# Row sums of |x − y| on one core: the final wait on the output store moves from SyncE to TensorE

## The chip, the cores and the metric

The kernel runs on one core of one Trainium2 chip. The metric is the device time of one execution in microseconds (us). The time of a kernel is the median of several executions without the profiler. One further execution is recorded by the hardware profiler; the profile and the trace come from that one.

## The reference

Two arrays of 1024 rows by 4096 columns are subtracted, and the absolute differences are summed along each row:

```python
def reference(x, y, axis):          # x, y: (1024, 4096) float32, axis = -1
    return np.sum(np.abs(x - y), axis=axis).astype(np.float32)
```

The output is 1024 numbers, 4 KB. The inputs are 33.5 MB.

## The kernel before

The 1024 rows are spread over the 128 partitions, so that each partition owns K = 8 rows. Rows 0 to 3 of a partition go through the buffers `xa` and `yb`; rows 4 to 7 go through `xb` and once more `yb`. VectorE (DVE) subtracts in place (L134), and ScalarE (ACT) takes the absolute value and sums along the row (L143) into one column of `ro`, the 128 by 8 tile of results. Rows 5 and 6 are handled in two halves each, and the last row in five pieces of 1728, 1024, 640, 384 and 320 columns, so that little work is left when the last bytes arrive. The last piece is done by VectorE alone: a subtraction (L175), and a sum over absolute values (L177) that adds the partial sums of the other pieces as well.

All input transfers but one are issued on SyncE's (SP's) queue, in the order of the code. The one exception, the first half of y, is issued by ScalarE (L114). Before each transfer that overwrites a row of `yb`, SP waits until VectorE has subtracted the row that stands there (L117 and L124).

The order on each engine is written out by hand. The helper `put` takes every instruction out of the block in which it was made. It either places it ahead of the program's first barrier (the first loads) or keeps it in the list `rest`, which is appended at the very end of the program, after the last barrier that the program itself has. So the program's barriers are all over within the first 2.4 us, and after that each engine simply runs its own list to the end. TensorE (PE) has nothing in that list: after the last barrier its program is over.

Every semaphore that the kernel counts up is also set back at the end by an instruction that waits for its final value and subtracts it. On VectorE `take_back` does this (L139). On SP three steps end the program:

- L183 and L184: SP waits until `s_end` has reached 7, that is, until all sums stand in `ro`, and issues the store of `ro` to the output. The store adds 16 to the semaphore `s_out` when it has landed.
- L185: SP sets `s_end` back.
- L186: SP waits until `s_out` has reached 16, and sets it back. Nothing follows it on SP.

Of the kernel before, what the change touches and what calls it, by code (L numbers as in the profile page):

```python
# [18 lines left out]
class Entry:  # L19
# [26 lines left out]
    def put(self, emit, before=None):  # L46

        nc = self.nc
        hook = nc.inst_callbacks[-1]
        lower = nc._always_lower_symbolic_ap  # L50
        nc.remove_inst_callback(hook)
        nc._always_lower_symbolic_ap = False
        n = len(nc.cur_bb.bb.instructions)
        try:
            emit()
        finally:
            nc._always_lower_symbolic_ap = lower
            nc.push_inst_callback(hook)
        here = nc.cur_bb.bb.instructions
        main = nc.main_func.blocks[0].instructions  # L60
        while len(here) > n:
            mine = here.pop(n)
            if before is None:
                self.rest.append(mine)
            else:
                first = next(i for i, x in enumerate(main) if x.engine == mine.engine and x.opcode == before)
                main.insert(first, mine)
# [3 lines left out]
def kernel(ctx, tc, x, y, axis, out):  # L71
    nc = tc.nc
# [11 lines left out]
    put = entry.put  # L84
# [24 lines left out]
    s_out = nc.alloc_semaphore("s_out")  # L109
# [73 lines left out]
    put(lambda: nc.sync.wait_ge(s_end, done))  # L183
    put(lambda: nc.sync.dma_start(out=orr, in_=ro).then_inc(s_out, 16))  # L184
    put(lambda: nc.sync.wait_ge(s_end, done).then_inc(s_end, -done))  # L185
    put(lambda: nc.sync.wait_ge(s_out, 16).then_inc(s_out, -16))  # L186


# [33 lines left out]
```

## Time and profile before

| what | us |
|---|---|
| median of 3 executions | 84.15 (84.14 to 84.20) |
| the profiled execution, its own time | 84.31 |
| its span, first to last recorded instruction of the kernel | 83.0 |
| VectorE busy | 36.4 |
| ScalarE busy | 31.6 |
| GpSimd (POOL) busy | 0.2 |
| mean rate of the transfers over the span | 404 GB/s |

The span begins with the first instruction that the kernel itself holds and ends with its last one. The device time of the same execution is longer by 1.3 us, which lies around the span; the page has no row for it. TensorE has no row of busy time because it does no matmul. An engine's letter with a q behind it (SPq, PEldq) means the engine's sequencer: waits, semaphore updates and the issuing of transfers.

### The profile page before, as it was taken

What the parts mean: (1) busy time and instruction counts of PE and PEld (TensorE: products, weight loads), DVE (VectorE), ACT (ScalarE), POOL (GpSimd) and SP (SyncE); (2) the same over time, 40 slices, a digit from 0 to 9 for tenths busy, and PEclk for the clock granted to TensorE, in tenths of its full rate; (3) what the DMA queues carried; (4) which work ended last, traced back from release to release, by engine and by line L of the source; (5) the groups of instructions that cost most, each with busy time, mean ns of one, the idle gap of its engine ahead of it and who ended that gap; (6) DMA issues with size and microseconds to landing.
All of it is one profiled execution on the core that took longest, in us unless ns stands there. A gap on an engine that the chain in (4) does not pass through costs nothing.

```text
span 83.0 us, 115 instructions
## 1 busy us (share of the span) xinstructions
DVE 36.4 (44%) x16; ACT 31.6 (38%) x27; POOL 0.2 (0%) x4
## 2 busy tenths in 40 slices
DVE  0000000000000000000199999999279898999772
ACT  0600000000000000000000979889790599999990
POOL 0000000000000000000000000000000000000000
DMA  6996899979798999998888999869999989999950
GB/s 126 411 735 269 379 569 498 434 332 553 332 521 363 490 395 403 498 403 379 379 379 379 450 663 403 379 253 395 474 395 419 466 379 419 423 411 409 405 207 2
DMA packets 2592, 33.56 MB, mean 404 GB/s; under 512 B 416, under 2 KB 928, under 8 KB 1696
## 3 DMA queue, kind: packets, MB, share of 16 engines
q1 hardware_dynamic: 2448, 25.17, 72.3%
q10 hardware_dynamic: 144, 8.39, 23.4%
HBM read 33.55 MB, written 0.00 MB: 404 GB/s over the span
## 4 chain that ended last, share of the span: by engine, by line
DMA 63%; DVE 17%; SPq 11%; issue 6%
DMA yb_rows<-in_y_dram 63%; DVE xa_rows L134 16%; SPq L122 6%; SPq L125 4%; DVE last_piece L175 1%; DVE ro_sums L177 1%
## 5 line engine op out<-in xcount | busy, mean ns | idle before, releaser
L134 DVE TENSOR_TENSOR xa_rows<-xa_rows,yb_rows 128x4096 f32<-128x4096 f32 x4 | 17.4, 4422 | 41.1 <-DMA yb_rows<-in_y_dram 41.1
L143 ACT ACTIVATE xa_rows<-xa_rows 128x4096 f32<-128x4096 f32 x4 | 14.5, 3616 | 43.8 <-DVE xa_rows L134 43.8
L134 DVE TENSOR_TENSOR xb_rows<-xb_rows,yb_rows 128x2048 f32<-128x2048 f32 (+5 forms) x9 | 17.9, 2016 | 3.6 <-DMA yb_rows<-in_y_dram 3.5
L143 ACT ACTIVATE xb_rows<-xb_rows 128x2048 f32<-128x2048 f32 (+1 forms) x5 | 11.2, 2245 | 3.0 <-DVE xb_rows L134 3.0
L143 ACT ACTIVATE abs_piece<-xb_rows 128x1728 f32<-128x1728 f32 (+3 forms) x4 | 3.8, 944 | 0.0
L143 ACT ACT_TABLE_LOAD x1 | 1.3, 1283 | 2.4 <-PEq L217 2.4
L143 ACT ACTIVATION_READ_ACCUMULATOR xb_rows<-xb_rows 128x1 f32 x5 | 0.9, 187 | 0.0
L143 ACT ACTIVATION_READ_ACCUMULATOR xa_rows<-xa_rows 128x1 f32 x4 | 0.7, 186 | 0.0
L143 ACT ACTIVATION_READ_ACCUMULATOR abs_piece<-xb_rows 128x1 f32 x4 | 0.7, 186 | 0.0
L175 DVE TENSOR_TENSOR last_piece<-xb_rows,yb_rows 128x320 f32<-128x320 f32 x1 | 0.5, 493 | 0.3 <-DMA yb_rows<-in_y_dram 0.3
L177 DVE TENSOR_REDUCE ro_sums<-last_piece 128x1 f32<-128x324 f32 x1 | 0.5, 491 | 0.0
L169 DVE TENSOR_REDUCE ro_sums<-half_sums 128x2 f32<-128x4 f32 x1 | 0.1, 150 | 0.0
L203 POOL MEMSET const-bfloat16-1.0<- 128x1 bf16 x1 | 0.1, 101 | 0.0
L203 POOL MEMSET const-uint8-127<- 128x1 uint8 x1 | 0.1, 101 | 0.0
L203 POOL MEMSET const-float32-0.0<- 128x1 f32 x1 | 0.1, 98 | 0.2 <-issue 0.2
L203 POOL MEMSET const-float32-1.0<- 128x1 f32 x1 | 0.1, 98 | 0.0
## 6 DMA issues: line engine op xcount, KB each, us to landing
xa_rows<-in_x_dram SPq DMA_DIRECT2D x1, 6144.0 KB, 36.9
xb_rows<-in_x_dram SPq DMA_DIRECT2D x1, 6144.0 KB, 53.3
yb_rows<-in_y_dram SPq DMA_DIRECT2D x3, 2048.0 KB, 15.5
xa_rows<-in_x_dram SPq DMA_DIRECT2D x1, 2048.0 KB, 17.0
xb_rows<-in_x_dram SPq DMA_DIRECT2D x1, 864.0 KB, 17.8
yb_rows<-in_y_dram SPq DMA_DIRECT2D x1, 864.0 KB, 15.9
xb_rows<-in_x_dram SPq DMA_DIRECT2D x1, 512.0 KB, 16.7
yb_rows<-in_y_dram SPq DMA_DIRECT2D x1, 512.0 KB, 17.5
```

The costliest lines, as they stand in the source:

```text
L122: put(lambda: nc.sync.dma_start(out=xb[:, H - 1, c], in_=xr[:, K - 1, c]).then_inc(s_piece[i], 16))
L125: put(lambda: nc.sync.dma_start(out=yb[:, H - 1, c], in_=yr[:, K - 1, c]).then_inc(s_piece[i], 16))
L134: put(lambda: nc.vector.tensor_sub(out=tx, in0=tx, in1=ty).then_inc(s_sub, 1))
L143: put(lambda: nc.scalar.activation(tx if out is None else out, tx, ABS, accum_out=to).then_inc(sem, 1))
L169: put(lambda: nc.vector.reduce_sum(out=ro[:, K - 3:K - 1], in_=half, axis=AX).then_inc(s_end, 1))
L175: put(lambda: nc.vector.tensor_sub(out=last[:, n_part:n_part + w], in0=tx, in1=ty).then_inc(s_end, 1))
L177: put(lambda: nc.vector.reduce_sum(out=ro[:, K - 1:K], in_=last, axis=AX, apply_absolute_value=True).then_inc(s_end, 1))
L203: nc = _bacc.Bacc("TRN2", target_bir_lowering=False, num_devices=1)
```

## The change

The last instruction, the wait for the store with the setting back of `s_out`, is given to TensorE. The store itself stays where it is, on SP's queue. SP's last instruction is then L185. TensorE's list, which was empty after the barriers, holds this one wait.

```diff
     put(lambda: nc.sync.wait_ge(s_end, done))
     put(lambda: nc.sync.dma_start(out=orr, in_=ro).then_inc(s_out, 16))
     put(lambda: nc.sync.wait_ge(s_end, done).then_inc(s_end, -done))
-    put(lambda: nc.sync.wait_ge(s_out, 16).then_inc(s_out, -16))
+    put(lambda: nc.tensor.wait_ge(s_out, 16).then_inc(s_out, -16))
```

In the built program nothing else differs: VectorE, ScalarE and GpSimd have the same instructions in the same order, SP has one fewer at its end, and TensorE one more at its end.

## The prediction

> **What bounds the kernel now.** I read the page's head, then the chain that ended last in order of time, then SP's own waits, and at the end the semaphore records of the trace, since the change touches only the last microsecond. The chain first (columns: start in us, length in us, what):
>
> ```profile
> 67.72 12.70 DMA yb_rows<-in_y_dram
> 80.42 0.02 issue
> 80.45 0.50 DVE last_piece L175
> 80.95 0.02 issue
> 80.97 0.49 DVE ro_sums L177
> ```
>
> The transfers set the time until 80.42, and two VectorE steps follow. Neither is touched by the change. After 81.46 only the store is left. From the timeline of the last stretch, SP's waits, the issues of transfers and the row of line L186:
>
> ```profile
> 81.49 0.35 SPq L184 DMA_DIRECT2D out_dram<-ro_sums  x1
> ```
> ```profile
> SPq L186 <- SPq L186: 1.1, 1, 1.1
> ```
> ```profile
> out_dram<-ro_sums SPq DMA_DIRECT2D x1, 4.0 KB, 1.4
> ```
> ```profile
> L186 SPq EVENT_SEMAPHORE  x1: 17/17/17, 83.0 to 83.0; - x1
> ```
>
> The store is issued at 81.49, lands 1.4 us later, and SP has waited 1.1 us for it when L186 ends the span. So the question is what follows once the store has landed. The span is 83.0 us and the same execution took 84.31: 1.31 us lie around the span, and the page says nothing of them.
>
> The trace does. It records updates of semaphores too, also by instructions that are not the kernel's. Semaphore 2 is none of the kernel's. Its updates from the kernel's own barriers on, with the last instruction of an engine that fits (us from the span's start; who made each is my reading):
>
> ```
>  2.592  first: TensorE or GpSimd, whose last instructions start at 2.306 and 2.253
> 80.931  ScalarE, whose last instruction ended at 80.817
> 80.969  GpSimd or TensorE, idle since 2.6
> 81.858  VectorE, whose last instruction started at 81.655
> 83.116  SP, whose L186 started at 82.957 and ended at 82.974
> 83.160  83.198  83.233  83.280                  four more, back down
> 84.068 84.102 84.140 84.184 84.208 84.306 84.344 84.378 84.425   the same again
> ```
>
> Five updates going up, four coming back: a chain in which each engine waits for the one ahead. SP is the last link, since only its update waits for the store. Between 83.237 and 83.843 some 230 other semaphores are updated once each, in five ranges of about fifty; the lowest range (7 to 53) starts at 83.497, last of the five, and ends at 83.843. Then a second chain of nine.
>
> [...] the second chain runs from 84.068 to 84.425, 357 ns for 8 hops. [...] here the 17 ns of L186 stand for a step of 159 ns up to SP's update.
>
> **The change, part by part.**
>
> Removed: L186 on SP. SP's list then ends with L185 at 81.89, so its closing steps (159 ns from L186's start to its chain update) go under the flight of the store. This saves nothing by itself, because SP may update only after VectorE, which waits for the engines ahead of it, and one of these is now TensorE.
>
> Added: one wait on TensorE. Nothing of the kernel is queued behind it, nobody in the kernel waits for it, no transfer is issued or moved, and TensorE is idle from 2.6 on. Its price comes from the barriers at the start, where both sequencers wait for the same release. The rows of line L217, filtered by engine:
>
> ```profile
> L217 PEldq EVENT_SEMAPHORE  x2: 51/51/51, 2.0 to 2.3; - x2
> ```
> ```profile
> L217 SPq EVENT_SEMAPHORE  x2: 17/17/17, 2.0 to 2.3; - x2
> ```
>
> The same wait takes 51 ns on TensorE and 17 on SP. In the third barrier the release is updated at 2.278, SP's wait starts at 2.294 and TensorE's at 2.306: TensorE reacts 28 ns after the update, SP 16. From the start of that wait to TensorE's chain update at 2.592 it is 286 ns, if the first link is TensorE. A second sign of its pace: in the second barrier its next instruction starts 151 ns after the wait, SP's 91.
>
> Moved: the place in the chain at which everyone waits for the store. Step by step, on the records of the profiled execution:
>
> 1. The sixteenth increment of `s_out` is at 82.940. [...] the records show sixteen increments, 82.740 to 82.940. The store stays as it was, so this stays.
> 2. TensorE's wait starts 28 ns later, 82.968 (SP's: 82.957, 17 ns after). **+0.011**
> 3. Its chain update comes 286 ns after that, 83.254 (SP's: 159 ns, 83.116). **+0.127**, together +0.138.
> 4. Before, four hops were left when the late engine updated: 83.280 − 83.116 = 0.164. Now, with TensorE first, all eight are left; the undisturbed chain shows them with 0.357. **+0.193**
> 5. From the first engine's release (83.280) to the last update (84.425) it is 1.145 us[...]. The lowest range ends last in both kernels and starts last, so this part moves as a block. **0**[...].
>
> Sum: 0.138 + 0.193 = **+0.331 us**, of which only about 0.045 (11 + 51 − 17 ns) shows as a longer span. The profiled execution goes from 84.31 to about 84.64. The median of 84.15 stands 0.16 below the profiled execution; I add the sum to it: **84.48**.
>
> Bounds of what I can't see. If the first link is GpSimd and TensorE the third, six hops are left: 0.044 + 0.024 + 0.098 + 0.038 + 0.034 + 0.047 = 0.285, so +0.121 in step 4 and +0.26 in all; I take first, since of the two TensorE is the slower and the first link reacts slowest in the way down (47 ns against 38). Step 3 could be as short as SP's 159 ns (then +0.20) and, with a second delay of 151 ns, as long as 437 (then +0.48).
>
> **The rivals.**
>
> *The time ends before the closing steps.* The last update is at 84.425 and the execution took 84.31, so one end of the metric isn't where my records begin or stop. If all of the 1.31 us lay ahead of the span, only the 0.045 us of the longer span would count: 84.20. Against it: nine updates follow within 84.07 to 84.43, hard to see left out of an 84.31 that starts near zero. For it: the page shows neither end.
>
> *SP's own closing work is what the tail consists of.* Then it would start at 81.91 rather than at 82.97, under the store, and the end would come sooner. It decides where SP's share of the tail, once it runs under the store, is longer than TensorE's by over 0.17 + 0.045. The gain is limited by L186's wait of 1.07 us; with half of that, less 0.045, it gives 84.15 − 0.49 = 83.66. Against it: after SP's update four hops follow that others make, and the highest range of semaphores, next to SP's place in the chain, is done at 83.330, half a microsecond ahead of the lowest.
>
> *The barrier is a count, not a chain.* Then only step 2 and step 3 count: +0.138, 84.29. Against it: gaps of 34 to 47 ns in the way down, and ScalarE's late update at 80.931, which drew the next 38 ns behind it.
>
> That the change doesn't do what it says is not open here: the built program has the wait on TensorE and nothing else moved.
>
> **How the numbers follow.** The chain with TensorE first or third: 0.80, between +0.20 and +0.48, likeliest +0.33. A count: 0.06, +0.14. The metric without the closing: 0.09, +0.05. SP's closing as the bound: 0.05, at 83.66. A measurement of this kernel can tell about 0.2%, 0.17 us, from no change. The chain is slower throughout; the count lies below that line and, with its own spread (0.1 to 0.25), gives 0.03 to each side of it. So faster 0.05, same 0.12, slower 0.83. The range runs from 84.20, which takes in the two small cases, to 84.62, just short of the longest step 3.
>
> **What would show it.** Right: L186 on TensorE with 51 ns, ending the span at about 83.02; SP's last instruction at 81.9; the updates of semaphore 2 not as 2.59, 80.93, 80.97, 81.86 and five late ones, but all nine after 83.2, within 0.36 us. Step 3 is read off the distance from the wait's start to the first of the nine, step 4 off the nine, step 5 off the distance from the ninth to the last. Wrong: one or more updates still ahead of the store beside a time that hasn't moved (TensorE is late in the chain), a store that lands later or sooner than 1.4 us, or nine late updates beside an unmoved time, which would put the metric's end before them.

## The result and the profile after

| | before | after |
|---|---|---|
| median, us | 84.15 (84.00 to 84.20, 6 executions) | 84.54 (84.39 to 84.73, 6 executions) |
| ratio | | 1.0052, 95% interval 1.0035 to 1.0068 |
| the profiled execution, us | 84.31 | 84.73 |
| its span, us | 82.97 | 83.07 |
| instructions in the span | 115 | 115 |

The change costs 0.39 us, about half a per cent. The six executions of the changed kernel include the profiled one, which was the longest; without it their median is 84.51. The span grew by only 0.09 us, and 0.05 of that is a later landing of the store; the rest of the cost lies behind the span. The end of the chain of waits in the kernel after (start in us, length in us, what):

```profile
67.76 12.71 DMA yb_rows<-in_y_dram
80.47 0.02 issue
80.49 0.51 DVE last_piece L175
81.00 0.02 issue
81.02 0.49 DVE ro_sums L177
```

These are the same steps with lengths equal within 0.01 us, all about 0.05 us later: the input transfers were that much later in this execution. SP's own waits, in the kernel after:

```profile
SPq L118 <- DVE xa_rows L134: 51.0, 3, 43.0
SPq L184 <- DVE ro_sums L177: 12.0, 1, 12.0
SPq L125 <- DVE xa_rows L134: 3.5, 1, 3.5
```

The row of L186 with its 1.1 us is gone from SP. The rows of lines L185 and L186 show where both now stand, and the timeline and the issues of transfers show the store:

```profile
L185 SPq EVENT_SEMAPHORE  x1: 17/17/17, 81.9 to 81.9; - x1
```
```profile
L186 PEldq EVENT_SEMAPHORE  x1: 51/51/51, 83.0 to 83.0; - x1
```
```profile
81.54 0.35 SPq L184 DMA_DIRECT2D out_dram<-ro_sums  x1
```
```profile
out_dram<-ro_sums SPq DMA_DIRECT2D x1, 4.0 KB, 1.4
```

SP is done at 81.9, TensorE's wait ends the span with its 51 ns, and the store takes 1.4 us as before. Nothing here accounts for 0.39 us. The records of semaphore 2, which is not the kernel's (its own instructions name only 96 to 112 in both traces), do (us from the span's start):

```
before   2.592 80.931 80.969 81.858 | 83.116 83.160 83.198 83.233 83.280
         84.068 84.102 84.140 84.184 84.208 84.306 84.344 84.378 84.425
after    | 83.346 83.380 83.419 83.463 83.486 83.584 83.624 83.658 83.704
         84.491 84.525 84.564 84.608 84.631 84.729 84.768 84.802 84.849
```

The bar marks the landing of the store, that is, the sixteenth increment of `s_out`: 82.940 before and 82.988 after. Before, four of the first nine updates had been made ahead of it. After, all nine follow it. From the landing to the last update it is 1.485 us before and 1.861 after, 0.376 more.

### The profile page after: what moved, and what is told of

Read it like the earlier page. It is cut to its first block, busy times and chain, and to the rows that moved or that the text cites. A ratio compares the mean times of both kernels' runs of the same rounds, so it can differ in the third digit from the quotient of the medians.

```text
span 83.1 us, 115 instructions
## 1 busy us (share of the span) xinstructions
DVE 36.4 (44%) x16; ACT 31.5 (38%) x27; POOL 0.2 (0%) x4
## 4 chain that ended last, share of the span: by engine, by line
DMA 63%; DVE 17%; SPq 10%; issue 6%
DMA yb_rows<-in_y_dram 63%; DVE xa_rows L134 16%; SPq L122 6%; SPq L125 4%; DVE last_piece L175 1%; DVE ro_sums L177 1%
```

## The experiments

The theory, read off the records above: at the end the engines pass a signal along a chain, TensorE first, then ScalarE, GpSimd, VectorE and SP, and back down to TensorE. What the wait on the store costs is set by the pace of the engine that holds it and by the links of the chain that are left after it. Rivals: using TensorE late costs by itself; only the engine's pace counts; or it costs that SP leaves while its store is under way.

The distances below are from the semaphore records of each profiled execution, in ns. An update is late when it is made after the landing of the store. "To wait" goes from the landing to the start of the wait on the store, "closing step" from there to the chain update that this engine makes, and "landing to last" from the landing to the very last update of semaphore 2; "against before" is the difference of the latter to the kernel before. Then come the medians' difference to before in the same comparison, and the ratio with its 95% interval.

The last column uses every execution. Each has a time, and a span that is known to 0.1 us. The difference of the two leaves out whatever happened ahead of the span's end, a late landing included. To its mean I add the part of the span that lies behind the landing in the profiled execution (34 ns before, 79 after), and subtract the same sum for the kernel before, 1.365 us over 102 executions in the later comparisons. The scatter of the difference makes the column good to some 0.02 us.

| run | late updates of the first nine | to wait | closing step | landing to last | against before | median, us | ratio | every execution, us |
|---|---|---|---|---|---|---|---|---|
| before | 5 | 17 | 159 | 1485 | | | | |
| after | 9 | 28 | 330 | 1861 | +376 | +0.39 | 1.0052 (1.0035 to 1.0068) | +0.39 |
| E1 TensorE early, SP waits | 5 | 17 | 148 | 1475 | −10 | −0.05 | 0.9997 (0.9985 to 1.0009) | −0.01 |
| E2 TensorE awake, and waits | 9 | 28 | 330 | 1862 | +377 | +0.41 | 1.0054 (1.0028 to 1.0079) | +0.37 |
| E3 ScalarE waits | 8 | 21 | 166 | 1654 | +169 | +0.19 | 1.0028 (1.0014 to 1.0042) | +0.18 |
| E4 VectorE waits | 6 | 27 | 204 | 1617 | +132 | +0.11 | 1.0014 (1.0001 to 1.0028) | +0.14 |
| E5 after again | 9 | 28 | 330 | 1863 | +378 | +0.43 | 1.0048 (1.0036 to 1.0060) | +0.39 |
| E6 TensorE, three more | 9 | 28 | 782 | 2313 | +828 | +1.14 | 1.0141 (1.0108 to 1.0173) | +0.82 |
| E7 SP, three more | 5 | 16 | 355 | 1680 | +195 | +0.23 | 1.0026 (1.0015 to 1.0037) | +0.20 |
| E8 TensorE and then SP | 9 | 28 | 330 | 1861 | +376 | +0.45 | 1.0059 (1.0045 to 1.0072) | +0.37 |
| E9 TensorE, two ahead | 9 | 28 | 286 | 1819 | +334 | +0.30 | 1.0037 (1.0021 to 1.0053) | +0.33 |
| E10 E6 again | 9 | 28 | 783 | 2315 | +830 | +0.80 | 1.0100 (1.0073 to 1.0127) | +0.81 |

In E6, E7 and E10 the closing step is counted from the first of the added waits; in E8 it is TensorE's. The two columns of differences that don't hold the landing, "against before" and "every execution", agree within 0.02 us in every row. The spare semaphore `s_pe` is allocated as in E1 wherever a later edit uses it; that line is not shown again.

**E1: TensorE has a last instruction, but an early one.** SP signals it after issuing the store.

```diff
+    s_pe = nc.alloc_semaphore("s_pe")
...
+    put(lambda: nc.sync.wait_ge(s_end, done).then_inc(s_pe, 1))
     put(lambda: nc.sync.wait_ge(s_end, done).then_inc(s_end, -done))
+    put(lambda: nc.tensor.wait_ge(s_pe, 1).then_inc(s_pe, -1))
     put(lambda: nc.sync.wait_ge(s_out, 16).then_inc(s_out, -16))
```

> The wait on the store is SP's again; TensorE gets a last instruction too, but one that is signalled by SP right after the store is issued, some 0.9 us before the store lands. Theory (a chain of engines, TensorE first, SP last; what counts is where in it the late engine stands, and how long its sequencer takes): TensorE's, ScalarE's, GpSimd's and VectorE's updates of semaphore 2 are all made by about 82.7 us, under the flight of the store, five updates are left after SP's wait, and the time is that of before, within 0.05 us. Rival (any last instruction on TensorE after its long idle time costs): +0.1 to +0.4 us, as in the changed kernel.

TensorE's row and SP's own wait in this run:

```profile
L188 PEldq EVENT_SEMAPHORE  x1: 51/51/51, 81.8 to 81.8; - x1
```
```profile
SPq L189 <- SPq L189: 1.0, 1, 1.0
```

TensorE's wait starts at 81.83 and makes its chain update at 82.159, and the next three follow by 82.275, all ahead of the landing at 82.836. SP still waits 1.0 us for the store. The time is that of before: an instruction on TensorE after its long idle time costs nothing here, where its chain update came 0.68 us ahead of the landing.

**E2: TensorE has worked just before.** As E1, but the wait on `s_out` is TensorE's too.

```diff
+    put(lambda: nc.sync.wait_ge(s_end, done).then_inc(s_pe, 1))
...
+    put(lambda: nc.tensor.wait_ge(s_pe, 1).then_inc(s_pe, -1))
-    put(lambda: nc.sync.wait_ge(s_out, 16).then_inc(s_out, -16))
+    put(lambda: nc.tensor.wait_ge(s_out, 16).then_inc(s_out, -16))
```

> As the changed kernel (TensorE waits for the store), but TensorE has one instruction ahead of it, signalled by SP just after the store is issued, so that its sequencer has worked within the last microsecond. Theory: still nine late updates in 0.36 us, so +0.33 to +0.38 us against before; what is open is the closing step of TensorE, 330 ns from its wait to its first update in the changed kernel against 286 in the kernel before, where it had just left a barrier: if the 80 us of waiting cost those 44 ns, it is 286 here, else 330. Rival (waking TensorE is most of the cost): the closing step falls by 0.15 us or more, and the time with it, to +0.2 us or less.

TensorE's two waits:

```profile
L188 PEldq EVENT_SEMAPHORE  x1: 51/51/51, 82.4 to 82.4; - x1
```
```profile
L189 PEldq EVENT_SEMAPHORE  x1: 51/51/51, 83.5 to 83.5; - x1
```

The second starts at 83.471, only 1.03 us after the first, and the chain update follows at 83.801. The closing step stayed at 330 ns. Long idleness of TensorE is not what costs, nor is it what separates 330 from 286.

**E3 and E4: the same wait on ScalarE, and on VectorE.** Each run has one of the two added lines.

```diff
-    put(lambda: nc.sync.wait_ge(s_out, 16).then_inc(s_out, -16))
+    put(lambda: nc.scalar.wait_ge(s_out, 16).then_inc(s_out, -16))    # E3
+    put(lambda: nc.vector.wait_ge(s_out, 16).then_inc(s_out, -16))    # E4
```

> The same wait is ScalarE's last instruction; TensorE has none. Theory: TensorE's update comes early again (2.6 us), eight come late. ScalarE's wait has SP's length, its closing step some 170 ns; from its update seven hops are left, 358 - 34 = 324 ns against SP's 164. So +0.15 us against before (the sequencer of ScalarE is fast: nearly all of it is its place). Rival (only the engine's own pace counts, not its place): within 0.03 us of before. Rival (it costs that SP leaves before its store has landed): the same 0.2 us on every engine other than SP, on top of the pace: +0.2.

> The same wait is VectorE's last instruction, behind the seven that set semaphores back. Theory: three updates come early, six late; VectorE's closing step is 203 to 231 ns (from its last instruction to its update in the kernel before), and from its update to the end of the chain it is 24 + 98 + 38 + 34 + 47 = 241 ns against SP's 164. So +0.13 us. Rival (pace alone): +0.055. Rival (SP leaving costs): +0.25.

The rows of the wait, first in E3, then in E4:

```profile
L186 ACTq EVENT_SEMAPHORE  x1: 17/17/17, 82.6 to 82.6; - x1
```
```profile
L186 DVEq EVENT_SEMAPHORE  x1: 21/21/21, 82.7 to 82.7; - x1
```

The first nine updates of semaphore 2 in these two runs, with the bar at the landing:

```
E3   2.583 | 82.788 82.827 82.870 82.893 82.991 83.031 83.065 83.112
E4   2.583 80.696 80.734 | 82.927 82.950 83.048 83.088 83.122 83.168
```

ScalarE's wait is as short as SP's, and its closing step only 7 ns longer. Yet the distance from landing to last is 169 ns longer, nearly all of it from ScalarE's update on: 324 ns to the end of the first pass (the first nine updates) instead of 164. That is place. Pace alone would have given 11 ns. VectorE is slower in pace but stands one link ahead of SP, and ends cheaper than ScalarE, at 132 ns. In E3 one of the nine updates came before the store, in E4 three, in the kernel after none: this shows the order TensorE, ScalarE, (GpSimd,) VectorE, SP. GpSimd has its place by elimination; the wait on GpSimd was not tried. The intervals of E3 and E4 overlap, so the medians would not tell the two apart. The last column, from 22 executions of each, does: +0.18 and +0.14.

**E5, E6, E7 and E10: the pace of the sequencer.** E5 is the changed kernel once more. E6 and E10 add three waits on TensorE that are satisfied once the store has landed. E7 adds the same three to the kernel before, on SP, ahead of SP's own last wait; all its lines have `nc.sync`.

```diff
+    for _ in range(2):
+        put(lambda: nc.tensor.wait_ge(s_out, 16).then_inc(s_pe, 1))     # E7: nc.sync
+    put(lambda: nc.tensor.wait_ge(s_pe, 2).then_inc(s_pe, -2))
     put(lambda: nc.tensor.wait_ge(s_out, 16).then_inc(s_out, -16))
```

> The changed kernel once more, beside before and the next three on one chip, for a narrower interval. Theory: +0.33 to +0.42 us; nine late updates of semaphore 2 within 0.36 us, the first 0.33 us after the start of TensorE's wait.

> The changed kernel with three more waits on TensorE that are satisfied as soon as the store has landed (two count a spare semaphore up, one sets it back). Theory (TensorE's sequencer lies open on the path after the store): three steps at the 151 ns that separate its instructions in the barriers, so 0.45 us more than the changed kernel, +0.83 us against before. Rival (the sequencer's pace is hidden, the cost is in the chain alone): no more than the changed kernel.

> The kernel before with the same three more waits, on SP. Theory: SP's sequencer lies open too, at 58 to 91 ns for a step: +0.17 to +0.27 us against before, clearly less than the same three on TensorE. Rival (time ends before the closing steps, or they are hidden): 0.

> The changed kernel with three more waits on TensorE after the landing, once more. In the first run of it the records from landing to last update gave 0.45 us more than the changed kernel, but the time was 1.1 us above before, with the store landing late. Theory (only the closing part differs, the late landing was chance): 2.313 us from landing to last update again, and a time of +0.7 to +0.95 us against before. Rival (the added waits delay the transfers too): the store lands about 0.5 us later than in the kernel before again, and +1.1 us or more.

The rows of the two waits of the loop, on TensorE in E10 and on SP in E7:

```profile
L188 PEldq EVENT_SEMAPHORE  x2: 51/51/51, 82.7 to 82.8; - x2
```
```profile
L188 SPq EVENT_SEMAPHORE  x2: 17/17/17, 83.2 to 83.2; - x2
```

TensorE's four waits start at 82.670, 82.821, 83.016 and 83.167: steps of 151, 195 and 151 ns. SP's start at 83.173, 83.247, 83.313 and 83.380: steps of 74, 66 and 67. TensorE's steps sum to 497 ns, but the closing step behind them is 286 instead of 330, so the three cost 0.45 us. SP's sum to 207 and cost 0.20 us: its closing step, too, is shorter here, 148 ns instead of 159. The medians of E10 (+0.80) and E7 (+0.23) agree with the records. The sequencers lie open on the path after the store, as expected. E6's median, +1.14, was more than the +0.83 of its records. What is too much lies ahead of the landing, which was at 83.506 in its profiled execution: its spans range from 83.2 to 84.2 us, while the time behind the landing is +0.82 over all six executions. E10, the same program, has the same distances within 2 ns, and landed the store at 82.642. So the added waits do not by themselves delay the transfers; why most executions of E6 had later transfers was not found.

**E8: SP stays until the store has landed, and TensorE is late as well.**

```diff
+    put(lambda: nc.tensor.wait_ge(s_out, 16).then_inc(s_pe, 1))
+    put(lambda: nc.sync.wait_ge(s_pe, 1).then_inc(s_pe, -1))
     put(lambda: nc.sync.wait_ge(s_out, 16).then_inc(s_out, -16))
```

> TensorE waits for the store and then signals SP, whose last instruction is the wait on the store as before; so SP does not leave before the store has landed, and TensorE is late as in the changed kernel. Theory: the chain begins with TensorE's update at the same distance from the store as in the changed kernel, SP is ready when the chain reaches it, so the time is that of the changed kernel within 0.05 us (+0.33 to +0.42). Rival (what costs is that SP leaves while its store is under way): at least 0.15 us less than the changed kernel.

The rows of TensorE's wait and of SP's last one in this run:

```profile
L187 PEldq EVENT_SEMAPHORE  x1: 51/51/51, 83.1 to 83.1; - x1
```
```profile
L189 SPq EVENT_SEMAPHORE  x1: 17/17/17, 83.2 to 83.2; - x1
```

SP ends last, as in the kernel before, and yet the distance from landing to last is the changed kernel's 1861 ns. That SP leaves early is not what costs.

**E9: where do TensorE's 44 ns come from?** Two short instructions ahead of TensorE's wait, both over before the store lands.

```diff
+    put(lambda: nc.sync.wait_ge(s_end, done).then_inc(s_pe, 1))
...
+    put(lambda: nc.tensor.wait_ge(s_pe, 1).then_inc(s_pe, 1))
+    put(lambda: nc.tensor.wait_ge(s_pe, 2).then_inc(s_pe, -2))
+    put(lambda: nc.tensor.wait_ge(s_out, 16).then_inc(s_out, -16))
```

> TensorE waits for the store as in the changed kernel, with two short instructions ahead of that wait, both done before the store lands. In the runs so far TensorE's closing step took 326 to 330 ns where its last instruction was the first or second after the barriers, and 285 or 286 where it was none or the fourth; and in the run with three more, the step from the second to the third took 195 ns beside 151 for its neighbours. Theory (one place in TensorE's instruction list, between the second and the third instruction after the barriers, costs 44 ns more, wherever the waits stand): here that place is passed under the store's flight, the closing step is 286 ns, and from the store's landing to the last update of semaphore 2 it is 1.818 us against 1.862 in the changed kernel and 1.485 in the kernel before. So +0.33 us against before. Rival (a wait that really waits costs the 44 ns): 330 ns and 1.862 us again, +0.38.

TensorE's three waits:

```profile
L188 PEldq EVENT_SEMAPHORE  x1: 51/51/51, 81.7 to 81.7; - x1
L189 PEldq EVENT_SEMAPHORE  x1: 51/51/51, 81.8 to 81.8; - x1
L190 PEldq EVENT_SEMAPHORE  x1: 51/51/51, 82.7 to 82.7; - x1
```

The third starts at 82.721, 28 ns after the landing, and the chain update is at 83.007. The closing step is 286 ns and the whole distance 1819, against 1818 expected: the extra 44 ns belong to a place in TensorE's list, not to waiting. What is at that place the runs don't show. SP seems to have such a place as well, with 8 to 11 ns: its closing step is 159 ns before, and 148 in E1 and E7, where more instructions stand ahead of it; and the first of its steps in E7 is 74 ns beside 66 and 67. No run was made for that.

No run beats the kernel before by more than a measurement tells. SP already is the last link, so with the wait on SP the fewest hops are left: four, 164 ns, against eight, 358 ns, with it on TensorE.

## Why the prediction was right

The forecast was +0.33 us and 84.48; measured were +0.39 and 84.54, within the range. The mechanism was the right one: a chain in which TensorE stands first, so that all of it now follows the store. The chain was a reading of the records before; the order on the way up is shown by E3, E4 and the kernel after, while the order on the way back down stays the author's reading. By its steps:

1. **The landing** was taken as unchanged. It came 48 ns later in the profiled execution after, and 29 ns earlier than before in E5: so this is the scatter of the transfers, no part of the change.
2. **TensorE's reaction**, 28 ns: measured 28 (82.988 to 83.016).
3. **TensorE's closing step**, 286 ns: measured 330. This is the mis-sized term. The 286 had been read where TensorE's list was empty after the barriers; with one instruction in it, the closing step passes the slow place, and the term is +0.171 instead of +0.127. With two instructions ahead, E9 gives the 286 back.
4. **Eight hops instead of four**, 0.357 us: measured 0.358. The four extra updates explain 0.14 of the 0.194; the other 0.054 is the sixth update, VectorE's by that reading, which takes 98 ns (83.486 to 83.584) when the chain comes up through VectorE, and took 44 before (83.116 to 83.160), when VectorE's own update lay 1.26 us ahead of SP's. The prediction had this in, since it took all eight hops from an undisturbed pass.
5. **From the first engine's release to the last update**, 1.145 us, moves as a block: measured 83.704 to 84.849, 1.145. The lowest range of the other semaphores (7 to 53) starts and ends last in both, 83.497 to 83.843 before and 83.920 to 84.267 after, so it starts 217 and 216 ns behind the ninth update.

Steps 2 to 5 with the measured closing step are 0.011 + 0.171 + 0.194 + 0 = 0.376 us, which is the difference of the landing-to-last distances. With the 48 ns of the later landing this gives 0.424, and the profiled executions differ by 0.42.

TensorE as the first link was the right choice over the third: all nine updates come late. The sign by which it was chosen, 47 ns against 38 on the way down, was thin; the third place would have given +0.26 us. The rival in which the time ends ahead of the closing steps is out: in every profiled run here the last update lies 0.113 to 0.122 us beyond the length of the execution, so the time moves with it, and E7 and E10 moved the time by steps that lie behind the landing. Where exactly the time begins and ends isn't shown. The rival with SP's own closing work as the tail is out by the kernel after, where SP was done 1.0 us ahead of the landing and nothing was gained, and by E8, where SP ended 0.2 us after the landing and nothing was lost. The rival of a plain count is out by E3, where an engine of SP's pace costs 169 ns through its place. What lies behind the ninth update has the same length in both kernels: the lowest range of the other semaphores takes 346 ns before and 347 after, and the second pass 357 (84.068 to 84.425) and 358 (84.491 to 84.849), in all these runs 356 to 358. The updates of the other semaphores together took 0.61 us before (83.237 to 83.843) and 0.66 after (83.604 to 84.267): the first of them comes 121 and 118 ns behind the fifth update, and the fifth lies 164 ns ahead of the ninth before and 218 after.

## What to carry to other kernels

Give the wait that ends last to the engine that is last in the closing chain (here SP: 1.485 us from the landing to the last update, against 1.617 on VectorE, 1.654 on ScalarE and 1.861 on TensorE), and let the engines ahead of it run out early, so that their part of the chain passes under that wait (in E1 by 82.275, ahead of the landing at 82.836). Among the engines tried in this program the choice was worth at most 0.38 us of 84 (TensorE against SP). The three waits added behind the last landing were paid at the pace of their sequencer: 207 ns of steps cost 195 on SP (E7), 497 cost 454 on TensorE (E10 against the kernel after), the shorter closing steps taken in. When a change moves the end of a program and the span hardly moves, read the semaphore records behind the last instruction, and measure from the landing of the last transfer rather than from the start. Once one trace has shown how much of the span lies behind the landing, time less span does the same for every execution.

## What was not expected of the hardware

- One step in TensorE's instruction list, between the second and the third after the barriers, takes 195 ns beside 151 for its neighbours (E6 and E10), and added 44 ns wherever it was passed after the landing (a closing step of 330 ns in the kernel after, E2, E5 and E8, beside 286 in E9).
- The closing part repeats within 2 ns (1861 to 1863 for the changed kernel, E5 and the two that should equal them, E2 and E8, 2313 and 2315 for E6 and E10), while the landing of the store wandered between 82.60 and 83.51 us over the profiled runs. Differences of 0.1 us are plain in the first and lost in the second.
- In an undisturbed pass the hop from the fifth update to the sixth (from SP back to VectorE, by the author's reading) takes 97 to 99 ns, every other hop 23 to 47. VectorE's own two updates then lie 121 or 122 ns apart (83.463 to 83.584 in the kernel after, 84.184 to 84.306 in the kernel before), near the 112 ns between the starts of its last two steps at L139 (81.543 and 81.655 in the kernel before). That its own pace sets this hop is a reading that no run here tests.
